# Reading the 256 activation columns of the feature-major products in turn from two halves

## The chip, the cores and the metric

The kernel runs on one core of a Trainium2 chip, in one launch. The metric is device time in microseconds, from single executions; a profile of one further execution shows which instruction ran when on each engine.

## The reference

One decoder layer on 256 tokens of width 2048, in float32:

```python
h = rms_norm(x, mix_pre_norm)
proj = h @ w_in                      # 2048 x 10536: RWKV-7, mLSTM and gate columns
merged = sigmoid(g_a) * (ha @ w_branch_a) + sigmoid(g_b) * (hb @ w_branch_b)
x = x + rms_norm(merged @ w_out, mix_post_norm)
x = x + rms_norm(cross_attention(rms_norm(x), rms_norm(mem), wq, wkv, wo), xattn_post_norm)
u = rms_norm(x) @ w_up               # 2048 x 16384, then a causal convolution over 3 tokens
x = x + rms_norm((gelu(gate) * up) @ w_down, ffn_post_norm)   # 8192 x 2048
```

Between `proj` and `merged` stand two recurrent mixers (an mLSTM and RWKV-7) of width 1024 each. Nearly all arithmetic is in the products with the weight matrices.

## The kernel before, in words

**Every large product is taken as three.** A float32 factor is split into a high part (rounded to the type fp32r) and a low part (the rest): x = xh + xl, w = wh + wl. The product is wh·xh + wh·xl + wl·xh. Activations are split once, by `split` and `split_gain` (lines 241 to 247: ScalarE makes the high part, VectorE the low one). Weights arrive by DMA on SyncE's queue in chunks of 128 partitions x 1024 columns, 512 KB each, into three buffers `raw`; `Feed.hi` makes `wh` on ScalarE (line 410) and `Feed.lo` makes `wl` on VectorE (line 432), each into one of four buffers.

**Two kinds of block.** In an "fm" (feature-major) block a 128x128 tile of weights is the stationary operand and the activations of all 256 tokens, 128x256, are the moving one; the result has features on partitions and tokens along the columns. Each product of 256 columns thus has a weight load of 128 columns of its own. A block has mostly 512 output columns: four tiles m, three products each, for each of 16 slices k of the input features. In a "tm" (token-major) block 128 tokens are the stationary operand and 512 weight columns the moving one (`tm_products`, line 436). The tm products read their 512 columns in turn from two halves already: `rearrange("p (a b) -> p b a", a=2)`, and the columns are paired on the host so that the result is in the natural order. The fm products read their 256 columns one after the other.

The fm blocks are: the small RWKV and gate columns (w_sm, 384 columns), r, k, v, q and the two gates (16 blocks of w_in), the two branches (8, with 8 slices k), w_mix_out (4), the keys and queries of the cross-attention (2), its output (4, with 4 slices k) and the feed-forward's first matrix (32). That is 144 + 54 x 192 + 8 x 96 + 4 x 48 = 11472 products of 256 columns. The tm blocks are mLSTM's v and o, the cross-attention's v and the feed-forward's second matrix.

**Where a weight chunk lies.** `Feed.staged` (line 367) places an fm chunk 16 elements into its buffer. In every second chunk ahead of the feed-forward's first matrix (and in one of 16, later one of 64, in it) the last 128 of its 1024 columns are set a further 8 elements on. Such a chunk is made by two instructions on each engine (896 and 128 columns) in place of one; `Feed.parts` and `Feed.tile` deal with the two pieces. A tm chunk lies at the start of its buffer.

**The order of work.** All instructions are written out in one program order. `run` walks through the blocks, chunk by chunk; the conversion of the next three chunks and the DMAs of the next six are issued ahead of a chunk's products. The results of a block are taken out of PSUM by generators (`r_evac`, `gate_evac`, `fu_evac` and so on), of which `Spread.half` runs a step between the slices of later blocks, by a budget of time for VectorE and ScalarE. The row scaling of the norm, `st0.rb` and its like (one number for each token, the same on all partitions), is multiplied in there, by a VectorE instruction that reads PSUM. An exception is the queries of mLSTM and the second half of `q_evac`, where 128^-0.5 goes in with it (`scalar_tensor_tensor`).

`keep_warm` issues products of a column of ones with itself; `Stat.row` and `Stat.column` are small products for the norms.

Of the kernel before, what the change touches and what calls it, by code (L numbers as in the profile page):

```python
# [10 lines left out]
F32R = mybir.dt.float32r  # L11
# [4 lines left out]
P = 128  # L16
# [136 lines left out]
def _layer(ctx, tc, nc, d, dbg):  # L153
# [194 lines left out]
    class Feed:  # L348
        def __init__(self):
            self.src = [s for b in blocks for s in b["srcs"]]  # L350
            self.kind = [b["kind"] for b in blocks for s in b["srcs"]]
            self.raw, self.st, self.nd, self.ns, self.nl = {}, {}, 0, 0, 0

            self.sm = wsm
# [31 lines left out]
        @staticmethod  # L386
        def parts(w, *others):

            if not isinstance(w, tuple):
                return [(w,) + others]  # L390
            n = w[0].shape[1]
            f = [o if isinstance(o, tuple) else o.rearrange("p k c -> p (k c)") for o in others]
            return [(w[0],) + tuple(o[0] if isinstance(o, tuple) else o[:, 0:n] for o in f),
                    (w[1],) + tuple(o[1] if isinstance(o, tuple) else o[:, n:] for o in f)]

        @staticmethod
        def tile(w, kj, nm, m):

            if not isinstance(w, tuple):
                return w[:, kj, m * P:(m + 1) * P]  # L400
            n = (kj * nm + m) * P
            return w[1] if n == w[0].shape[1] else w[0][:, n:n + P]

        def hi(self, upto):
            while self.ns <= min(upto, len(self.src) - 1):
                self.dma(self.ns)
                r = self.raw[self.ns]
                wh = self.staged("wh", r, self.ns)
                for h, v in self.parts(wh, r):
                    nc.scalar.copy(h, v)  # L410
                self.st[self.ns] = [wh, None]
                self.ns += 1

        def first(self):

            r, wh, wl = self.raw.pop(0), self.staged("wh", self.src[0], 1), self.staged("wl", self.src[0], 1)
            nc.vector.tensor_copy(wh[:, 0], r[:, 0])
            for kj in range(2):
                x_split(0, kj)
                if kj:  # L420
                    nc.scalar.copy(wh[:, 1], r[:, 1])  # L421
                nc.vector.tensor_sub(wl[:, kj], r[:, kj], wh[:, kj])
            self.st[0] = [wh, wl]
            self.ns = self.nl = 1

        def lo(self, upto):
            self.hi(upto)
            while self.nl <= min(upto, len(self.src) - 1):
                r = self.raw.pop(self.nl)
                wl = self.staged("wl", r, self.nl)  # L430
                for l, v, h in self.parts(wl, r, self.st[self.nl][0]):
                    nc.vector.tensor_sub(l, v, h)  # L432
                self.st[self.nl][1] = wl
                self.nl += 1
# [9 lines left out]
    def run():  # L444
# [6 lines left out]
        for b in blocks:  # L451
# [14 lines left out]
            for ci, s in enumerate(b["srcs"]):  # L466
# [12 lines left out]
                for kj in range(s.shape[1]):  # L479
                    xh, xl = b["xs"](k) if kj else ahead  # L480
                    first, last = k == 0, k == nk - 1
                    if b["kind"] == "fm":
                        for m in range(nm):
                            o = banks[second * 2 + m // 2][:, m % 2]
                            a, c = feed.tile(wh, kj, nm, m), feed.tile(wl, kj, nm, m)
                            mm(o, a, xh, start=(first and m % 2 == 0), stop=False)
                            if not (b["two"] and ci == 0 and first):
                                mm(o, a, xl, start=False, stop=False)
                            mm(o, c, xh, start=False, stop=last)
                        if b["two"] and ci == 0 and first:  # L490

                            for m in range(nm):
                                mm(banks[m // 2][:, m % 2], feed.tile(wh, kj, nm, m), xl, start=False, stop=False)
# [10 lines left out]
            if nt:  # L504
# [9 lines left out]
                for g, o in enumerate(banks):  # L514
                    for si, (w, kj, xh, xl) in enumerate(steps):
# [3 lines left out]
                        for m in range(2 if b["kind"] == "fm" else 0):  # L519
                            a, c = (feed.tile(v, kj, nm, g * 2 + m) for v in w)  # L520
                            mm(o[:, m], a, xh, start=(b["bankwise"] and si == 0 and m == 0), stop=False)
                            mm(o[:, m], a, xl, start=False, stop=False)
                            mm(o[:, m], c, xh, start=False, stop=si == len(steps) - 1)
                        if si % 2:
# [62 lines left out]
    def sm_evac(ps):  # L587
# [6 lines left out]
        pr = PR()  # L594
        dve.tensor_mul(pr, ps[0], bc(st0.rb, 2))
        wa, gl = C("wa", "m0"), T2("gl")
# [4 lines left out]
        pr = PR()  # L601
        dve.tensor_mul(pr[:, 0], ps[1][:, 0], st0.rb)
        shiftmix(gl1, pr[:, 0], 26, slice(0, 32))
# [173 lines left out]
    def k_evac(hf):  # L777
        def gen(ps):
# [4 lines left out]
            for g in range(2):  # L783
                pr = PR()
                dve.tensor_mul(pr, ps[g], bc(st0.rb, 2))
                yield
# [135 lines left out]
    def v_evac(hf):  # L922
        def gen(ps):
            if hf == 0:
                M["vT"], M["vt"] = U("vT"), U("vt", [P, 2, 1024])
            for g in range(2):
                p0 = hf * 4 + g * 2
                pr = PR()
                dve.tensor_mul(pr, ps[g], bc(st0.rb, 2))
                yield  # L930
# [164 lines left out]
    def q_evac(i):  # L1095
        def gen(ps):
# [4 lines left out]
            for g in range(2):  # L1101
                o = qk[:, i * 4 + g * 2:i * 4 + g * 2 + 2]
                if i == 0:
                    dve.tensor_mul(o, ps[g], bc(st0.rb, 2))
                else:
                    dve.scalar_tensor_tensor(o, ps[g], 128 ** -0.5, bc(st0.rb, 2), op0=ALU.mult, op1=ALU.mult)
                yield
            if i == 1:
# [33 lines left out]
    def mlstm():  # L1142
# [40 lines left out]
        for k2 in range(4):  # L1183
# [5 lines left out]
            for j in range(2):  # L1189
                k = k2 * 2 + j  # L1190
                split_gain(ha[0][:, k], ha[1][:, k], q[:, j], pcol("hn", k))
            yield

    def hb_split():
# [16 lines left out]
        for p2 in range(4):  # L1211
# [17 lines left out]
            dve.tensor_mul(M["bv"][:, s2], M["bv"][:, s2], q)  # L1229
            split(hb[0][:, s2], hb[1][:, s2], M["bv"][:, s2])  # L1230
            yield


    def gate_evac(i, cb):
        def gen(ps):
            sg = [T2("sg") for _ in range(2)]
            M["sg", i, cb] = sg
            for g in range(2):
                dve.tensor_mul(sg[g], ps[g], bc(st0.rb, 2))
                act.activation(sg[g], sg[g], AF.Sigmoid)  # L1240
                yield
        return gen

    def br_evac(i, cb):
        def gen(ps):
# [5 lines left out]
            for g in range(2):  # L1251
# [4 lines left out]
                else:  # L1256
                    dve.tensor_mul(sg[g], ps[g], sg[g])
                    dve.tensor_add(sg[g], sg[g], pa)
                    split(M["mg"][0][:, s2], M["mg"][1][:, s2], sg[g])
                yield  # L1260
# [29 lines left out]
    class Residual:  # L1290
# [11 lines left out]
        def run(self):  # L1302
# [165 lines left out]
    def kx_evac(ps):  # L1468
        M["kT"] = [T2("kT") for _ in range(2)]
        for g in range(2):  # L1470
            dve.tensor_mul(M["kT"][g], ps[g], bc(stm.rb, 2))
        yield
# [65 lines left out]
    def xo():  # L1538
        M["oT"] = U("oT", [P, 2, 4, S], F32R)
        for h2 in range(2):  # L1540
            q = aux("xo", [P, 2, S])
            for j in range(2):
                h = h2 * 2 + j
                for mt in range(2):
                    mm(q[:, j], M["xv"][mt][:, h * P:(h + 1) * P], M["pT", h][:, mt], start=(mt == 0), stop=(mt == 1))
            split(M["oT"][:, 0, h2 * 2:h2 * 2 + 2], M["oT"][:, 1, h2 * 2:h2 * 2 + 2], q)
            yield
# [298 lines left out]
```

## Time and profile before

| | |
|---|---|
| median of 3 executions | 1861.94 us (1861.43 to 1862.66) |
| the profiled execution | 1859.39 us |
| its span, first to last instruction | 1857.6 us |
| TensorE, its weight loads | 1843.2 us busy (99%), 1774.6 us (96%) |
| VectorE, ScalarE, GpSimd | 1313.3 us (71%), 1034.0 us (56%), 30.6 us (2%) |
| DMA | 352.73 MB, mean 190 GB/s |

The span is the time from the first to the last instruction, and the profiled execution's own time is 1.8 us longer. Matmuls are pipelined: one is listed with 276 ns, yet the next begins some 113 ns after it. So the busy share of TensorE says only that it never stopped; what counts is the time from the start of one product to the start of the next, called the pitch below. It is got from a merged row by dividing its length by its count.

### The profile page before, as it was taken

How to read it: one execution, taken by the hardware profiler on the slowest of the kernel's cores; microseconds unless marked ns; L12 is line 12 of the kernel's file. 1: busy time of each engine (PE TensorE's matmuls, PEld its weight loads, DVE VectorE, ACT ScalarE, POOL GpSimd, SP SyncE). 2: the span in 40 equal slices, each digit the busy share in tenths (PEclk: the TensorE clock that was granted, in tenths of full speed). 3: DMA queues.
4: the chain of work that ended last, by engine and by line, in shares of the span. 5: the costliest groups of instructions: out<-in, count | busy, mean ns of one | idle time of the engine just before them, and what ended most of it. 6: DMA issues, size and time to landing. Idle time of an engine off the chain costs nothing.

```text
span 1857.6 us, 36660 instructions
## 1 busy us (share of the span) xinstructions
PE 1843.2 (99%) x15038; PEld 1774.6 (96%) x15038; DVE 1313.3 (71%) x1957; ACT 1034.0 (56%) x1619; POOL 30.6 (2%) x53
## 2 busy tenths in 40 slices
PE   9999999999999999999999999999999999999998
PEld 9999988999999999899999999999999998888887
DVE  6879985765765767768777777666677676666665
ACT  6687455554544665665555655554554455555553
POOL 0100000100100000000000000000000000000000
PEclk9999999999999999999999999999999999999999
DMA  7656555354556675545666566666666666666664
GB/s 255 195 180 182 161 186 154 111 175 148 175 181 203 222 245 174 190 143 186 200 198 195 188 193 196 200 193 195 193 194 193 193 192 207 225 204 204 204 204 159
DMA packets 97913, 352.73 MB, mean 190 GB/s; under 512 B 11057, under 2 KB 11313, under 8 KB 97361
## 3 DMA queue, kind: packets, MB, share of 16 engines
q1 hardware_dynamic: 96496, 348.07, 59.9%
q8 instruction: 117, 1.92, 0.4%
q0 software_dynamic: 384, 1.18, 0.3%
q10 hardware_dynamic: 864, 1.15, 0.2%
q14 instruction: 52, 0.42, 0.1%
HBM read 347.73 MB, written 2.10 MB: 188 GB/s over the span
## 4 chain that ended last, share of the span: by engine, by line
PE 95%; DVE 3%; issue 1%; ACT 0%; DMA 0%; POOL 0%; DVEq 0%; POOLq 0%; SPq 0%; ACTq 0%
PE fm L188 68%; PE tm L188 23%; DVE wl L432 1%; PE gram L188 0%; PE Y L188 0%; DVE ql L66 0%; PE lv L188 0%; DVE z L66 0%; PE num L188 0%; PE X L188 0%; PE zwa L188 0%; DMA wsm<-in_w_sm_dram 0%; PE U L188 0%; PE gramA L188 0%; PE xo L188 0%
## 5 line engine op out<-in xcount | busy, mean ns | idle before, releaser
L432 DVE TENSOR_TENSOR wl<-raw,wh 128x1024 fp32r<-128x1024 f32 (+2 forms) x756 | 789.1, 1058 | 416.2 <-ACT wh L410 413.5
L410 ACT CAST wh<-raw 128x1024 fp32r<-128x1024 f32 (+2 forms) x756 | 678.7, 915 | 511.6 <-PE fm L188 332.0
L188 PE MATMUL fm<-fh,wh 128*128 128x256 f32 x2048 | 565.6, 276 | 0.6 <-ACT fh L66 0.6
L188 PE MATMUL fm<-fh,wl 128*128 128x256 f32 x2048 | 565.8, 276 | 0.4 <-DVE wl L432 0.4
L188 PE MATMUL fm<-fl,wh 128*128 128x256 f32 x2048 | 564.9, 276 | 0.0
L188 PEld LDWEIGHTS fm<-fh,wl 128*128 128x128 f32 x2048 | 384.5, 188 | 1.0 <-DVE wl L432 0.6
L188 PEld LDWEIGHTS fm<-fh,wh 128*128 128x128 f32 x2048 | 384.5, 188 | 0.8 <-ACT fh L66 0.8
L188 PEld LDWEIGHTS fm<-fl,wh 128*128 128x128 f32 x2048 | 384.3, 188 | 0.0
L188 PE MATMUL tm<-wh,as 128*128 128x512 f32 x1024 | 304.6, 379 | 0.0
L188 PE MATMUL fm<-hh,wh 128*128 128x256 f32 x1072 | 301.3, 281 | 1.3 <-ACT wh L421 1.3
L188 PE MATMUL fm<-hh,wl 128*128 128x256 f32 x1072 | 297.8, 278 | 0.3 <-DVE wl L432 0.2
L188 PE MATMUL fm<-hl,wh 128*128 128x256 f32 x1072 | 297.6, 278 | 0.0
L188 PEld LDWEIGHTS tm<-wh,as 128*128 128x128 f32 x1024 | 193.5, 189 | 27.4
L188 PEld LDWEIGHTS fm<-hh,wh 128*128 128x128 f32 x1072 | 201.6, 188 | 3.4 <-ACT hh L66 1.6
L188 PEld LDWEIGHTS fm<-hh,wl 128*128 128x128 f32 x1072 | 201.6, 188 | 0.7 <-DVE wl L432 0.4
L188 PEld LDWEIGHTS fm<-hl,wh 128*128 128x128 f32 x1072 | 201.7, 188 | 0.2
L188 PE MATMUL tm<-wl,as 128*128 128x512 f32 x512 | 194.0, 379 | 0.0
L188 PEld LDWEIGHTS tm<-wl,as 128*128 128x128 f32 x512 | 96.8, 189 | 13.7
L66 ACT CAST as<-ac 128x256 fp32r<-128x256 f32 x128 | 45.5, 403 | 103.7 <-PE tm L188 103.7
L66 DVE TENSOR_TENSOR as<-ac,as 128x256 fp32r<-128x256 f32 x128 | 48.6, 422 | 52.6 <-ACT as L66 52.5
L188 PE MATMUL fm<-mgh,wh 128*128 128x256 f32 x256 | 71.0, 277 | 0.0
L188 PE MATMUL fm<-mgh,wl 128*128 128x256 f32 x256 | 70.9, 277 | 0.0
(361 smaller groups left out, 2150.2 us busy)
## 6 DMA issues: line engine op xcount, KB each, us to landing
raw<-in_w_fu_dram SPq DMA_DIRECT2D x256, 512.0 KB, 4.2
raw<-in_w_in_dram SPq DMA_DIRECT2D x160, 512.0 KB, 3.9
raw<-in_w_fd_dram SPq DMA_DIRECT2D x128, 512.0 KB, 4.1
raw<-in_w_br_dram SPq DMA_DIRECT2D x32, 512.0 KB, 4.0
raw<-in_w_mo_dram SPq DMA_DIRECT2D x32, 512.0 KB, 4.2
raw<-in_w_xk_dram SPq DMA_DIRECT2D x8, 512.0 KB, 4.3
raw<-in_w_xq_dram SPq DMA_DIRECT2D x8, 512.0 KB, 3.6
raw<-in_w_xv_dram SPq DMA_DIRECT2D x8, 512.0 KB, 3.9
```

What stands on the lines that cost most here:

```text
L66: return f(out, *a, **k)
L188: pe.matmul(out, lhsT, rhs, start=start, stop=stop, skip_group_check=True)
L410: nc.scalar.copy(h, v)
L432: nc.vector.tensor_sub(l, v, h)
```

## The change

The moving operand of the fm products is read in turn from two halves of 128 columns (`turns`): columns 0, 128, 1, 129 and so on. For the result to have its tokens in the natural order, either the activations are stored so that the even tokens lie in the first half and the odd ones in the second, or the result is put in order when it is taken out of PSUM. Where activations are made for fm products alone (the branches' inputs, the merged mixers, the residual stream's splits, the attention's output) their splits read the source with a step of two elements and write one half after the other (`xsplit`, `xsplit_gain`, `Residual.parts`). The first norm's output `hh`, `hl` and the memory's `mh`, `ml` also serve the tm products, so they stay in the natural order and the evacuations of their fm products reorder (`times`). The feed-forward's evacuation `fu_evac` is untouched, since its input comes from `Residual.parts`. In `q_evac` both halves go by `times`, and the factor 128^-0.5 moves to the later product with `pw`. Weight chunks lie at the start of their buffer, in one piece; `parts`, `tile` and the list `kind` are gone.

```diff
+    def halves(ap):
+        return ap.rearrange("p k (b a) -> p k a b" if len(ap.shape) == 3 else "p (b a) -> p a b", a=2)
+    def apart(ap):
+        return ap.rearrange("p k (a b) -> p k a b" if len(ap.shape) == 3 else "p (a b) -> p a b", a=2)
+    def turns(ap):
+        return ap.rearrange("p (a b) -> p b a", a=2)
+    def xsplit(hi, lo, src):
+        split(apart(hi), apart(lo), halves(src))
+    def xsplit_gain(hi, lo, src, g):
+        split_gain(apart(hi), apart(lo), halves(src), g)
+    def times(out, ps, row):
+        if len(ps.shape) == 3:
+            row = bc(row, ps.shape[1])
+        dve.tensor_mul(apart(out), halves(ps), apart(row))
...
-        def staged(self, name, r, i):
+        def staged(self, name, r):
+            w = wp.tile([P, 1024 + 128], F32R, tag=name, bufs=4, name=name)
             k, c = r.shape[1:]
-            up = i - len(self.src) + 384
-            o = gap = 0
-            if self.kind[i] == "fm":
-                o = 16
-                if up < 0:
-                    gap = 0 if i % 2 else 8
-                elif i % (16 if up < 80 else 64) == 0:
-                    gap = 8
-            w = wp.tile([P, 1024 + 128], F32R, tag=name, bufs=4, name=name)
-            if gap:
-                n = o + k * c - P
-                return w[:, o:n], w[:, n + gap:n + gap + P]
-            return w[:, o:o + k * c].rearrange("p (k c) -> p k c", k=k)
+            return w[:, 0:k * c].rearrange("p (k c) -> p k c", k=k)
...
-                for h, v in self.parts(wh, r):
-                    nc.scalar.copy(h, v)
+                nc.scalar.copy(wh, r)
...
-                for l, v, h in self.parts(wl, r, self.st[self.nl][0]):
-                    nc.vector.tensor_sub(l, v, h)
+                nc.vector.tensor_sub(wl, r, self.st[self.nl][0])
...
                     if b["kind"] == "fm":
+                        xh, xl = turns(xh), turns(xl)
...
-                dve.tensor_mul(pr, ps[g], bc(st0.rb, 2))
+                times(pr, ps[g], st0.rb)
...
-                    dve.tensor_mul(M["pw"][:, h], M["pw"][:, h], q)
+                    dve.scalar_tensor_tensor(M["pw"][:, h], q, 128 ** -0.5, M["pw"][:, h], op0=ALU.mult, op1=ALU.mult)
...
-                split_gain(ha[0][:, k], ha[1][:, k], q[:, j], pcol("hn", k))
+                xsplit_gain(ha[0][:, k], ha[1][:, k], q[:, j], pcol("hn", k))
...
-                    act.activation(hi[:, k], part(xr, i)[:, j], AF.Identity, scale=pcol(gname, k))
+                    act.activation(apart(hi[:, k]), halves(part(xr, i)[:, j]), AF.Identity, scale=pcol(gname, k))
...
-                    dve.scalar_tensor_tensor(lo[:, k], part(xr, i)[:, j], pcol(gname, k), hi[:, k],
+                    dve.scalar_tensor_tensor(apart(lo[:, k]), halves(part(xr, i)[:, j]), pcol(gname, k), apart(hi[:, k]),
                                              op0=ALU.mult, op1=ALU.subtract)
```

The other evacuations (`sm_evac`, `k_evac`, `v_evac`, `q_evac`, `gate_evac`, `kx_evac`) and splits (`hb_split`, `br_evac`, `xo`) change in the same way.

More of the change, by code (lines that the diff above doesn't have):

```diff
@@ L350, in __init__ @@
             self.src = [s for b in blocks for s in b["srcs"]]
-            self.kind = [b["kind"] for b in blocks for s in b["srcs"]]
             self.raw, self.st, self.nd, self.ns, self.nl = {}, {}, 0, 0, 0
@@ L365, in dma @@
                 self.nd += 1
-        def staged(self, name, r, i):
+        def staged(self, name, r):
+            w = wp.tile([P, 1024 + 128], F32R, tag=name, bufs=4, name=name)
             k, c = r.shape[1:]
-            up = i - len(self.src) + 384
-            o = gap = 0
-            if self.kind[i] == "fm":
-                o = 16
-                if up < 0:
-                    gap = 0 if i % 2 else 8
-                elif i % (16 if up < 80 else 64) == 0:
-                    gap = 8
-            w = wp.tile([P, 1024 + 128], F32R, tag=name, bufs=4, name=name)
-            if gap:
-                n = o + k * c - P
-                return w[:, o:n], w[:, n + gap:n + gap + P]
-            return w[:, o:o + k * c].rearrange("p (k c) -> p k c", k=k)
[L386 to L402, printed above, removed]
+            return w[:, 0:k * c].rearrange("p (k c) -> p k c", k=k)
         def hi(self, upto):
@@ L414, in first @@
         def first(self):
-            r, wh, wl = self.raw.pop(0), self.staged("wh", self.src[0], 1), self.staged("wl", self.src[0], 1)
+            r, wh, wl = self.raw.pop(0), self.staged("wh", self.src[0]), self.staged("wl", self.src[0])
             nc.vector.tensor_copy(wh[:, 0], r[:, 0])
@@ L482, in run @@
                     if b["kind"] == "fm":
+                        xh, xl = turns(xh), turns(xl)
                         for m in range(nm):
                             o = banks[second * 2 + m // 2][:, m % 2]
-                            a, c = feed.tile(wh, kj, nm, m), feed.tile(wl, kj, nm, m)
+                            a, c = (w[:, kj, m * P:(m + 1) * P] for w in (wh, wl))
                             mm(o, a, xh, start=(first and m % 2 == 0), stop=False)
@@ L492, in run @@
                             for m in range(nm):
-                                mm(banks[m // 2][:, m % 2], feed.tile(wh, kj, nm, m), xl, start=False, stop=False)
+                                mm(banks[m // 2][:, m % 2], wh[:, kj, m * P:(m + 1) * P], xl, start=False, stop=False)
                     else:
@@ L519, in run @@
                         for m in range(2 if b["kind"] == "fm" else 0):
[L520 to L523, printed above, removed]
+                            a, c = (v[:, kj, (g * 2 + m) * P:(g * 2 + m + 1) * P] for v in w)
+                            mm(o[:, m], a, turns(xh), start=(b["bankwise"] and si == 0 and m == 0), stop=False)
+                            mm(o[:, m], a, turns(xl), start=False, stop=False)
+                            mm(o[:, m], c, turns(xh), start=False, stop=si == len(steps) - 1)
                         if si % 2:
@@ L594, in sm_evac @@
         pr = PR()
-        dve.tensor_mul(pr, ps[0], bc(st0.rb, 2))
+        times(pr, ps[0], st0.rb)
         wa, gl = C("wa", "m0"), T2("gl")
@@ L601, in sm_evac @@
         pr = PR()
-        dve.tensor_mul(pr[:, 0], ps[1][:, 0], st0.rb)
+        times(pr[:, 0], ps[1][:, 0], st0.rb)
         shiftmix(gl1, pr[:, 0], 26, slice(0, 32))
@@ L784, in gen @@
                 pr = PR()
-                dve.tensor_mul(pr, ps[g], bc(st0.rb, 2))
+                times(pr, ps[g], st0.rb)
                 yield
@@ L928, in gen @@
                 pr = PR()
-                dve.tensor_mul(pr, ps[g], bc(st0.rb, 2))
+                times(pr, ps[g], st0.rb)
                 yield
@@ L1102, in gen @@
                 o = qk[:, i * 4 + g * 2:i * 4 + g * 2 + 2]
[L1103 to L1106, printed above, removed]
+                times(o, ps[g], st0.rb)
                 yield
@@ L1229, in hb_split @@
             dve.tensor_mul(M["bv"][:, s2], M["bv"][:, s2], q)
-            split(hb[0][:, s2], hb[1][:, s2], M["bv"][:, s2])
+            xsplit(hb[0][:, s2], hb[1][:, s2], M["bv"][:, s2])
             yield
@@ L1238, in gen @@
             for g in range(2):
-                dve.tensor_mul(sg[g], ps[g], bc(st0.rb, 2))
+                times(sg[g], ps[g], st0.rb)
                 act.activation(sg[g], sg[g], AF.Sigmoid)
@@ L1258, in gen @@
                     dve.tensor_add(sg[g], sg[g], pa)
-                    split(M["mg"][0][:, s2], M["mg"][1][:, s2], sg[g])
+                    xsplit(M["mg"][0][:, s2], M["mg"][1][:, s2], sg[g])
                 yield
@@ L1470, in kx_evac @@
         for g in range(2):
-            dve.tensor_mul(M["kT"][g], ps[g], bc(stm.rb, 2))
+            times(M["kT"][g], ps[g], stm.rb)
         yield
@@ L1545, in xo @@
                     mm(q[:, j], M["xv"][mt][:, h * P:(h + 1) * P], M["pT", h][:, mt], start=(mt == 0), stop=(mt == 1))
-            split(M["oT"][:, 0, h2 * 2:h2 * 2 + 2], M["oT"][:, 1, h2 * 2:h2 * 2 + 2], q)
+            xsplit(M["oT"][:, 0, h2 * 2:h2 * 2 + 2], M["oT"][:, 1, h2 * 2:h2 * 2 + 2], q)
             yield
```

4 lines of the change are left out of this document (2 added, 2 removed).

## The prediction

> **What bounds the kernel now.** I read the page first, then the chain of waits in order of time, then the groups by form, then short stretches of the timeline.
>
> ```profile
> PE 1843.2 (99%) x15038; PEld 1774.6 (96%) x15038; DVE 1313.3 (71%) x1957; ACT 1034.0 (56%) x1619; POOL 30.6 (2%) x53
> ...
> PEclk9999999999999999999999999999999999999999
> ...
> PE 95%; DVE 3%; issue 1%; ACT 0%; DMA 0%; POOL 0%; DVEq 0%; POOLq 0%; SPq 0%; ACTq 0%
> ```
>
> The chain that ended last is TensorE for 95%, at its full granted clock throughout. So the time is the number of products times their pitch, plus about 5% of waits. The chain, in order of time, gives the pitch by stage (start, length, what, count):
>
> ```profile
> 35.32 37.24 PE fm L188 x324
> ...
> 354.96 20.73 PE fm L188 x180
> ...
> 519.15 145.24 PE fm L188 x1272
> ...
> 818.50 44.05 PE fm L188 x384
> ...
> 896.93 620.97 PE fm L188 x5470
> 1517.90 327.65 PE tm L188 x1518
> ```
>
> The feed-forward's fm products go at 620.97/5470 = 113.5 ns. The four pieces before it sum to 247.26 us for 2160, 114.5 ns, with single pieces up to 115.2. The tm products, of twice the columns, go at 327.65/1518 = 215.8 ns, and half of that is 107.9. So 256 columns cost an fm product at least 5.6 ns more than they cost a tm product. Two things differ: an fm product has a weight load for every 256 columns, not 512, and it reads its columns in sequence, where the tm product reads in turn from two halves.
>
> The matmul's own length tells something too (mean ns of one):
>
> ```profile
> L188 PE MATMUL fm<-fh,wl 128*128 128x256 f32 x2048 | 565.8, 276 | 0.4 <-DVE wl L432 0.4
> L188 PEld LDWEIGHTS fm<-fh,wl 128*128 128x128 f32 x2048 | 384.5, 188 | 1.0 <-DVE wl L432 0.6
> ...
> L188 PE MATMUL tm<-wl,hh 128*128 128x512 f32 x128 | 48.5, 379 | 0.0
> ...
> L188 PEld LDWEIGHTS tm<-wl,hh 128*128 128x128 f32 x128 | 24.2, 189 | 3.4
> ```
>
> The load is as long beside a product that reads in turn (189) as beside one that reads in sequence (188): reading in turn does not hold up the load. And these tm rows have the operands of the fm blocks with the roles changed, hh as weights and wl moving, with wl at the start of its buffer.
>
> **Do load and moving read disturb each other?** At the tile that is set 8 elements apart (matmul starts, in a w_in block):
>
> ```profile
> 158.70 0.28 PE L188 MATMUL fm<-hh,wl 128*128 128x256 f32 x1
> 158.81 0.28 PE L188 MATMUL fm<-hh,wh 128*128 128x256 f32 x1
> 158.93 0.28 PE L188 MATMUL fm<-hl,wh 128*128 128x256 f32 x1
> 159.06 0.28 PE L188 MATMUL fm<-hh,wl 128*128 128x256 f32 x1
> 159.18 0.28 PE L188 MATMUL fm<-hh,wh 128*128 128x256 f32 x1
> 159.29 0.28 PE L188 MATMUL fm<-hl,wh 128*128 128x256 f32 x1
> ```
>
> The steps are 110, 120, 130, 120, 110 ns, and such a bump returns every 48 products, that is two chunks. Only the place of the weights changes there, so where the weights lie against the moving read sets the pitch. My reading: a sequential read goes through its 256 columns at twice the rate of a load through its 128, so the two cross while both run; read in turn, the moving operand goes through two ranges of 128 columns, at the rate of the load, and does not cross it.
>
> The Trainium skill, "TensorE: Matmul & The Clock Gate", section "Step-by-step: what each phase is for", says that the moving operand and the weight load have independent read ports and that loading takes nothing from the running matmul. By that rule nothing would be there to gain (the third case below); the bump speaks against it.
>
> **What is left when they no longer cross** is the load alone or the 256 columns alone, whichever is longer. The load alone shows where a product has one moving column; the pair, where both operands are one broadcast column:
>
> ```profile
> 319.25 0.97 PEld L188 LDWEIGHTS den<-ones,pw 128*128 128x128 f32 x8
> ...
> 816.82 1.06 PE L188 MATMUL warm<-ones 128*128 128x128 f32 x8
> ...
> 259.93 1.04 PE L981 MATMUL bkt<-con,BK 128*128 128x128 f32 x8
> ```
>
> Eight loads in 0.97 us with 0.19 for the last: 0.78/7 = 111.4 ns. The eight warm products, with some 0.27 for the last, 0.79/7 = 113 ns (rows are rounded to 10 ns, so 111 to 114). The transposes, 0.77/7 = 110 ns. I take **111.5 ns**, the load's own row, as the new pitch. The bounds are 107.9 (half a tm product, no load in the way) and 113.5 (nothing gained).
>
> **The change part by part, against the profiled execution's 1859.39 us.**
>
> Pitch. There are 144 + 54 x 192 + 8 x 96 + 4 x 48 = 11472 fm products by the blocks. Of these 5470 at 113.5 come to 111.5: 5470 x 2.02 = 11.0 us. The other 6002 at 114.5: 6002 x 2.97 = 17.8 us. Nothing lies beside them that would hide this, since they are the chain. Together -28.9 us. Products of tm blocks and of the mixers stay.
>
> Chunks in one piece.
>
> ```profile
> L432 DVE TENSOR_TENSOR wl<-raw,wh 128x1024 fp32r<-128x1024 f32 x524 | 640.3, 1223 | 341.6 <-ACT wh L410 339.6 <-PE fm L188 1.2
> ...
> L432 DVE TENSOR_TENSOR wl<-raw,wh 128x896 fp32r<-128x896 f32 x116 | 126.4, 1089 | 74.6 <-ACT wh L410 73.8
> ...
> L410 ACT CAST wh<-raw 128x128 fp32r<-128x128 f32 x116 | 34.1, 294 | 0.0
> L432 DVE TENSOR_TENSOR wl<-raw,wh 128x128 fp32r<-128x128 f32 x116 | 32.9, 284 | 0.0
> ```
>
> 116 chunks save 1089 + 284 - 1223 = 150 ns on VectorE, 17 us in all, and on ScalarE somewhat under the 294 of its second piece. This lies beside TensorE; I count it as nothing, at most 1 us where VectorE is late (below).
>
> Reordering. The changed instructions read or write with a step of 8 bytes, which no row shows. The rows bound it:
>
> ```profile
> L66 ACT COPY Lt<-L x2: 1122/1128/1134, 255.3 to 257.2; 128x512 f32<-128x512 f32 x2
> ...
> L66 ACT CAST mgh<-sg 128x512 fp32r<-128x512 f32 x8 | 5.0, 622 | 20.4 <-DVE sg L66 20.4
> ...
> L66 DVE TENSOR_TENSOR mt<-cmt,con 128x256 f32<-128x256 f32 x8 | 5.1, 631 | 0.0
> ...
> L66 DVE SCALAR_TENSOR_TENSOR ql<-xr,par,qh 128x256 fp32r<-128x256 f32 x16 | 7.1, 479 | 0.2 <-ACT qh L66 0.2
> ...
> 36.00:218.00 182.00, 182.00 (x1651) 179.44 (x1650) 156.04 (x279) 117.82 (x200) 12.76 (x21) 1.00 0.61 180
> ...
> 720.00:766.00 46.00, 45.66 (x375) 44.46 (x373) 40.94 (x67) 28.54 (x47) 0.70 (x1) 1.00 0.56 175
> ```
>
> With a step of 128 bytes a ScalarE copy of 512 takes 1128 ns against 622, and a VectorE product of 256 that reads so takes 631, 152 more than ql's 479. So each 256 elements cost between 0 and some 250 ns more. 8 bytes are nearest to the contiguous rows: I take 0. On VectorE 49 instructions of 512 change (35 `times`, 14 splits) and 41 of 256: at the dear end 49 x 0.5 + 41 x 0.25 = 35 us over the kernel, less the 17 saved. TensorE covers that wherever VectorE has room. In these windows (busy us of PE, PEld, DVE, ACT, POOL with counts) VectorE has 156 of 182 us in r, k and v. It lacks room only from 720 to 766 us: 40.9 busy of 46, and there stand 16 ql and 2 kT. Dear, these add 20 x 0.25 = 5 us, and VectorE (46) would pass TensorE (45.7, less 1): a loss of 1 to 3 us. If VectorE is late, the waiting wl holds the product queue of TensorE. `oT`'s first split runs beside the second half of its own xo products, 1.9 us of cover against 1.3 now.
>
> The factor moved in `q_evac` swaps one VectorE form for another, four times; nothing. No DMA and no wait is added; each chunk's DMAs are issued at the same place.
>
> Sum: 1859.4 - 28.9 = 1830.5 us. The median of before is 2.55 us above its profiled execution, so 1833 us against the median.
>
> **The rivals.**
>
> *The 256 columns bound, not the load.* Then the pitch is between 107.9 and 110, take 109: 5470 x 4.5 + 6002 x 5.5 = 57.6 us, 1804 us. For it: the transposes' 110. Against: their load is another row than fp32r's, and den's 111.4 is the closest to an fm load.
>
> *Nothing to gain in the steady pitch.* If 113.5 is the load of these weights itself, only the bumps go: 6002 x 0.97 = 5.8 us, 1856 us, and with dear reordering it is within the measurement. For it: warm's 113. Against: den.
>
> *Slower: the new place is a bad one.* Without the 16 elements and the steps of 8, the weights may lie so that load and moving read hinder each other all along. The products of the mixer's gate, whose operands lie elsewhere, show such a pitch:
>
> ```profile
> 502.56 0.40 PE L188 MATMUL zg<-gs,gwh 128*128 128x256 f32 x2
> ...
> 503.52 0.28 PE L188 MATMUL fm<-hh,wh 128*128 128x256 f32 x1
> ```
>
> Eight in 0.96 us, 120 ns. All fm products so: 5470 x 6.5 + 6002 x 5.5 = 68.6 us, 1931 us. It decides from a mean pitch of 114 upward. Against it stand the tm rows above, read in turn with wl at the start of its buffer, 379 and 189 ns.
>
> *Slower still: each column of the other half pays.* A matmul whose columns cost double is there:
>
> ```profile
> 321.66 1.03 PE L188 MATMUL num<-vm,pw 128*128 128x256 f32 x4
> ```
>
> With 0.38 for the last, 0.65/3 = 217 ns; for 11472 products 1.18 ms more, about 3.0 ms. The tm products jump between halves 1024 bytes apart and pay nothing at 215.8 for 512; the fm halves are 512 bytes apart, which no row shows. The Trainium skill, "SBUF — State Buffer", section "Door 1: The DMA port swizzle", says that an access that leaves its 16-byte line pays; by that rule every column would. The tm rows contradict it here.
>
> **How the numbers follow.** Forecast 1833 us: 0.53. Columns bound: 0.13. Only the bumps: 0.16. A bad place: 0.15. Doubled columns: 0.03. The first three hold 0.82, so the range goes from 1803 to 1859, which takes in dear reordering (+3 on 1856). A measurement of this kernel can tell about 0.2%, 3.7 us. Faster by more: 0.53 + 0.13 + 0.11 of the third = 0.77; the rest of it, 0.05, within; slower 0.18.
>
> **What would show it.** The feed-forward's row of the chain: 5470 products in 610 us if right, 621 if nothing is gained, 656 if the place is bad. Matmuls of fm listed with fewer than 276 ns, and no bumps. The wl group has one form, 640 of 1024 columns near 1223 ns. Rows of `sg`, `pr` and `ql` near 684, 683 and 479 ns say that reordering is free. The stretch around 720 to 766 us would show VectorE on the chain if not. I am wrong if the pitch stays while loads become shorter, or if the load's row grows above 192.

## The result and the profile after

| | before | after |
|---|---|---|
| median (4 executions each) | 1862.0 us | 1838.92 us (1838.59 to 1839.28) |
| ratio | | 0.9876, 95% interval 0.9859 to 0.9893 |
| profiled execution, its span | 1859.39, 1857.6 us | 1839.28, 1837.5 us |

The change saves 1.2%, some 23 us; the two profiled executions are 20.1 us apart, and the accounts below go by these.

First the page of the kernel after: busy time by engine, and the chain that ended last.

```profile
PE 1821.2 (99%) x15038; PEld 1752.7 (95%) x15038; DVE 1305.5 (71%) x1838; ACT 1025.9 (56%) x1500; POOL 30.6 (2%) x53
...
PE 95%; DVE 2%; issue 1%; ACT 1%; DMA 0%; POOL 0%; DVEq 0%; POOLq 0%; SPq 0%; ACTq 0%
```

The same number of matmuls, nearly the same shares: over the whole span nothing else became the bound. The chain in order of time has nearly the same pieces as before:

```profile
34.91 36.18 PE fm L188 x324
...
349.38 20.30 PE fm L188 x180
...
510.12 142.05 PE fm L188 x1272
...
808.71 43.35 PE fm L188 x384
...
892.03 605.72 PE fm L188 x5422
1497.75 327.65 PE tm L188 x1518
```

The fm products go at 605.72/5422 = 111.7 ns in the feed-forward, from 113.5. At 36.18/324 = 111.7 ns and 142.05/1272 = 111.7 ns the early blocks, from 114.9 and 114.2, now have the same pitch: there are no bumps left. The piece of 384 has 112.9, with breaks in it. The one of 180 has 112.8 by length and count, but its products start 111 or 112 ns apart all through; its length takes in the end of the last one. The tm piece is the same to 0.01 us.

The groups by form that answer to those of before (busy us, mean ns of one):

```profile
L422 DVE TENSOR_TENSOR wl<-raw,wh 128x1024 fp32r<-128x1024 f32 x640 | 780.8, 1223 | 405.8 <-ACT wh L401 399.3
...
L188 PE MATMUL fm<-fh,wl 128*128 128x256 f32 x2048 | 563.5, 275 | 0.8 <-DVE wl L422 0.8
...
L188 PEld LDWEIGHTS fm<-fh,wl 128*128 128x128 f32 x2048 | 393.3, 192 | 1.4 <-DVE wl L422 1.4
...
L66 DVE TENSOR_TENSOR sg<-fm,st_b 128x512 f32<-128x512 f32 x16 | 10.9, 684 | 0.1
L66 DVE TENSOR_TENSOR pr<-fm,st_b 128x512 f32<-128x512 f32 x13 | 8.9, 683 | 0.0
L66 ACT ACTIVATE qh<-xr,par 128x256 fp32r<-128x256 f32 x16 | 8.8, 593 | 10.7 <-DVE xr L66 10.7
L66 DVE SCALAR_TENSOR_TENSOR ql<-xr,par,qh 128x256 fp32r<-128x256 f32 x16 | 7.4, 499 | 0.3 <-ACT qh L66 0.3
L66 ACT CAST mgh<-sg 128x512 fp32r<-128x512 f32 x8 | 6.3, 792 | 21.2 <-DVE sg L66 21.2
```

Three readings. The load is listed with 192 ns in place of 188, which is also the length of most loads of `den` before; this alone does not say that the load is the bound now, as the run in sequence below shows. The evacuations that reorder what they read from PSUM (`sg`, `pr`) cost the same as before: their two lines stand in the view of before with the same figures. The splits that reorder from SBUF are dearer on ScalarE (`mgh` 792 against 622) and hardly on VectorE (`ql` 499 against 479).

### The profile page after: what moved, and what is told of

Read it like the earlier page. It is cut to its first block, busy times and chain, and to the rows that moved or that the text cites. A ratio compares the mean times of both kernels' runs of the same rounds, so it can differ in the third digit from the quotient of the medians.

```text
span 1837.5 us, 36430 instructions
## 1 busy us (share of the span) xinstructions
PE 1821.2 (99%) x15038; PEld 1752.7 (95%) x15038; DVE 1305.5 (71%) x1838; ACT 1025.9 (56%) x1500; POOL 30.6 (2%) x53
## 4 chain that ended last, share of the span: by engine, by line
PE 95%; DVE 2%; issue 1%; ACT 1%; DMA 0%; POOL 0%; DVEq 0%; POOLq 0%; SPq 0%; ACTq 0%
PE fm L188 67%; PE tm L188 23%; DVE wl L422 1%; PE gram L188 0%; PE Y L188 0%; DVE ql L66 0%; PE lv L188 0%; PE num L188 0%; ACT wh L401 0%; PE X L188 0%; PE zwa L188 0%; DMA wsm<-in_w_sm_dram 0%; PE U L188 0%; PE gramA L188 0%; DMA raw<-in_w_xv_dram 0%
## 5 line engine op out<-in xcount | busy, mean ns | idle before, releaser
L422 DVE TENSOR_TENSOR wl<-raw,wh 128x1024 fp32r<-128x1024 f32 x640 | 780.8, 1223 | 405.8 <-ACT wh L401 399.3
L401 ACT CAST wh<-raw 128x1024 fp32r<-128x1024 f32 x640 | 667.1, 1045 | 502.2 <-PE fm L188 281.7
L188 PEld LDWEIGHTS fm<-fh,wl 128*128 128x128 f32 x2048 | 393.3, 192 | 1.4 <-DVE wl L422 1.4
L188 PEld LDWEIGHTS fm<-fh,wh 128*128 128x128 f32 x2048 | 393.4, 192 | 0.1
L188 PEld LDWEIGHTS fm<-fl,wh 128*128 128x128 f32 x2048 | 393.0, 192 | 0.0
L188 PEld LDWEIGHTS fm<-hh,wh 128*128 128x128 f32 x1072 | 206.5, 193 | 3.3 <-ACT hh L66 1.5
L188 PEld LDWEIGHTS fm<-hh,wl 128*128 128x128 f32 x1072 | 206.6, 193 | 0.2 <-DVE wl L413 0.2
L188 PEld LDWEIGHTS fm<-hl,wh 128*128 128x128 f32 x1072 | 206.5, 193 | 0.1
```

The costliest lines, as they stand in the source:

```text
L188: pe.matmul(out, lhsT, rhs, start=start, stop=stop, skip_group_check=True)
L401: nc.scalar.copy(wh, r)
L422: nc.vector.tensor_sub(wl, r, self.st[self.nl][0])
```

## The experiments

The theory: the sequential moving read and the weight load hinder each other by an amount that depends on where the weights lie; in turn from two halves they do not, and then the load alone sets the pitch. Rivals: the gain comes from the chunks' new place or from their being in one piece; the 256 columns, not the load, set the new pitch. All of these run on the changed kernel with the edit shown. Except for two, each time is that of a single execution; the kernel before, executed beside them, has medians from 1859.5 to 1861.5 us.

### In sequence at the new place

```diff
-        return ap.rearrange("p (a b) -> p b a", a=2)
+        return ap.rearrange("p (a b) -> p b a", a=1)
```

(and the same in `halves` and `apart`)

> The changed kernel, but the fm products read their 256 columns in sequence again (one part in place of two halves; splits and evacuations in natural order); chunks stay in one piece at the start of their buffer. If reading in turn is what helps, the fm pitch goes back to 113.4 ns at least, and, without the 16 elements and the steps of 8, perhaps to the 117 to 123 ns of the bumps: 1860 us or more, up to 1930. If the chunks' place or their being in one piece is what helps, the pitch stays near 111.7 ns: 1839 us.

Measured: 1926.98 us, 88 us above the changed kernel and 66 above the kernel before. The feed-forward's piece of the chain:

```profile
898.62 686.87 PE fm L188 x5724
```

and two groups by form:

```profile
L188 PE MATMUL fm<-fh,wl 128*128 128x256 f32 x2048 | 579.4, 283 | 0.0
...
L188 PEld LDWEIGHTS fm<-fh,wl 128*128 128x128 f32 x2048 | 393.3, 192 | 0.0
```

686.87/5724 = 120.0 ns, and each matmul is listed 7 ns longer than before. So the new place is a bad one for a sequential read, and the whole gain is the reading in turn. The load is listed with 192 ns here too, though loads follow each other 120.0 ns apart: its length does not tell what bounds. The 16 elements and the steps of 8 of the kernel before did something: without them its fm products would go much as in this run.

### In turn at the old place

The class `Feed` and the calls of `tile` are those of before; the rest is the changed kernel.

> The changed kernel with the old place of the chunks (16 elements in, last tile 8 further on in every second chunk of the early blocks, made in two pieces). If reading in turn makes the place irrelevant, the fm pitch is 111.7 ns with no bumps: 1839 us, or 1 to 2 us more where VectorE is late. If the place matters still, bumps of 117 to 123 ns come back every 48 products: 1845 us or more.

Measured: 1838.72 us, the same as the changed kernel. The feed-forward's piece:

```profile
891.50 605.72 PE fm L188 x5422
```

605.72 us for 5422, to the digit that of the changed kernel, and over all stages the products go at 111 or 112 ns with no bump. So with the halves in turn it makes no difference at which of the two places the weights lie. And making 116 chunks in two pieces costs nothing on the chain. (On VectorE it is 17 us by the listed lengths, but the busy time of its `wl` group is only 7.4 us longer, 788.2 against 780.8 us.)

### In sequence, 16 elements in

```diff
-            return w[:, 0:k * c].rearrange("p (k c) -> p k c", k=k)
+            return w[:, 16:16 + k * c].rearrange("p (k c) -> p k c", k=k)
```

(on top of the run in sequence)

> As the run in sequence, but the fm chunks (and here the tm chunks too) lie 16 elements into their buffer, with no last tile set apart. If the 16 elements are what kept the sequential read at 113.4 ns before, the undisturbed feed-forward shows 113.4 ns again where the run at the start of the buffer shows more. If not, both show the same pitch.

Measured: 1884.73 us. The feed-forward's piece of the chain:

```profile
898.45 644.78 PE fm L188 x5470
```

117.9 ns in the feed-forward: better than at the start of the buffer (120.0) and worse than before (113.5). So the 16 elements are a part of it, and the last tile set 8 elements apart the larger one. In the trace of this run some stretches stay at 113 and others at 118 ns, as this piece of earlier blocks (113.4 ns) beside the one above:

```profile
520.80 111.45 PE fm L188 x983
```

It happens within one block too: in the feed-forward the products start 113 ns apart until a wait at 904 us, and 118 ns apart from there to the end. So this read has two steady states, and there nothing brings it back to the better one. I had read the bumps of before as a cost of the step of 8. By the starts in the trace of before they also put the pitch back: after the one at 129 us it stays at 118 ns, and the next, at 135.6 us, puts it back to 113.

### Short products, short loads

```diff
-                                mm(o, a, xl, start=False, stop=False)
+                                mm(o[:, 0:P], a, xl[:, 0:64], start=False, stop=False)
```

> The changed kernel, where the product wh times xl takes only 128 of its 256 columns (the low part of half the tokens' activations is left out; the blocks that are done bank by bank keep theirs). One third of the fm products then streams half as long. If the weight load sets the pitch of 111.7 ns, nothing changes: 111.7 ns for all three products, 1839 us. If the 256 columns set it, the short ones fall towards 56 ns: some 3700 products x 50 ns, 180 us less.

Measured: 1838.47 us, no difference. The groups by form:

```profile
L188 PE MATMUL fm<-fh,wl 128*128 128x256 f32 x2048 | 671.7, 328 | 0.9 <-DVE wl L422 0.8
L188 PE MATMUL fm<-fl,wh 128*128 128x128 f32 x2044 | 453.8, 222 | 0.0
...
L188 PEld LDWEIGHTS fm<-fl,wh 128*128 128x128 f32 x2048 | 393.0, 192 | 0.0
```

and the feed-forward's piece of the chain:

```profile
891.22 605.72 PE fm L188 x5422
```

One third of the products stream half as long, and 5422 of them still take 605.72 us: what the short product leaves free, the next one takes longer (328 ns in place of 275). So the 256 columns do not set the pitch.

```diff
-                                mm(o, a, xl, start=False, stop=False)
+                                mm(o[0:64], a[:, 0:64], xl, start=False, stop=False)
```

> The changed kernel, where the product wh times xl loads only 64 of its 128 weight columns (the low part's product is left out for half the features; the blocks that are done bank by bank keep theirs). If the load sets the pitch, the step that waits for the short load falls from 111.7 ns to what 256 columns take alone, 108 to 110 ns, one third of the products: 3700 x 2 to 4 ns, 7 to 14 us less. If the columns set it already, nothing changes: 1839 us.

Measured: 1829.89 us, 9.0 us less. The short load's group by form:

```profile
L188 PEld LDWEIGHTS fm<-fl,wh 128*64 128x64 f32 x2044 | 282.1, 138 | 0.0
```

and the feed-forward's piece of the chain:

```profile
887.20 601.20 PE fm L188 x5422
```

601.20/5422 = 110.9 ns on average. With two steps at 111.7 the third, the one that waits for the short load, is at 109.2; the starts in the trace agree, with two steps of three at 111 or 112 ns and one at 109 or 110. So the load sets the pitch and the 256 columns would allow 109.2: 2.5 ns per product are left, for whoever finds a way to load less often. I did not find one.

### Why two halves?

My theory had a mechanism: two halves make the moving read go through its places at the load's rate, so that they never cross. Four kernels test it.

```diff
-        return ap.rearrange("p (a b) -> p b a", a=2)
+        return ap.rearrange("p (a b) -> p b a", a=4)
```

(and in `halves` and `apart`)

> Four quarters in turn in place of two halves (columns 0, 64, 128, 192, 1, 65 and so on), splits with a step of four. If what matters is only that load and moving read do not run at different rates through the same places, two halves are special: with quarters the moving read goes at half the load's rate, they cross again, and the pitch is above 111.7 ns, 113 or more. If it matters only that neighbouring columns come from different places, quarters do as well: 111.7 ns in the feed-forward, with ScalarE's and VectorE's splits of step 16 bytes dearer than those of step 8 (qh 593 ns, ql 499 ns).

Measured: 2153.63 us. The feed-forward's piece of the chain:

```profile
1026.04 786.10 PE fm L188 x5724
```

and the group of one form:

```profile
L188 PE MATMUL fm<-fh,wl 128*128 128x256 f32 x2048 | 618.4, 302 | 0.0
```

786.10/5724 = 137.3 ns in the feed-forward, far above the sequential read, and 143.3 in the early blocks (185.76 us for 1296). In turn is not good as such.

```diff
-        return ap.rearrange("p (a b) -> p b a", a=2)
+        return ap.rearrange("p (h a b) -> p h b a", h=2, a=2)
```

(here and in the next two with a=1 in `halves` and `apart`, so without any reordering)

> The changed kernel with another order of reading: first columns 0 to 127 in turn from their halves of 64 (0, 64, 1, 65 and so on), then columns 128 to 255 the same way. Activations are stored and results taken out in the natural order, so the tokens of every fm result stand in another order than the reference's; the work is the same. Two places at a time, 256 bytes apart, each gone through at the load's rate; the quarters had four places, 256 bytes apart, each at half that rate. If two places at the load's rate are what counts, the pitch is 111.7 ns. If 256 bytes apart is what made the quarters dear, it is 130 ns or more. If the jump in the middle meets the load, something between, 113 to 125 ns.

Measured: 1836.46 us; its feed-forward piece is again 605.72 us for 5422, 111.7 ns. So places 256 bytes apart, the quarters' distance, are not what made them dear.

```diff
-        return ap.rearrange("p (a b) -> p b a", a=2)
+        return ap[:, 0:P].unsqueeze(2).broadcast_to((P, P, 2))
```

> No reordering, and the fm products read the first 128 columns in sequence, each twice in a row (0, 0, 1, 1 and so on); the other half of the tokens is left out and the first half stands twice. One place only, gone through at the load's rate. If the rate is what counts, one place does as well as two: 111.7 ns, 1836 to 1839 us. If it is that neighbouring columns come from different places, the pitch is that of the sequential read at this place, 120 ns: 1925 us.

Measured: 1840.64 us, 111.7 ns. One place at the load's rate does as well as two: that neighbouring columns come from different places is not the point.

```diff
-        return ap.rearrange("p (a b) -> p b a", a=2)
+        return ap.rearrange("p (a b) -> p b a", a=2)[:, 0:64].unsqueeze(2).broadcast_to((P, 64, 2, 2))
```

> No reordering, and the fm products read two places in turn, each column pair twice (0, 128, 0, 128, 1, 129 and so on up to 63 and 191); half of the tokens is left out and the others stand twice. Two places, each gone through at half the load's rate, as the quarters' four were. If the rate is what made the quarters dear, the pitch is above 111.7 ns here too, 115 to 143. If it is the number of places, 111.7 ns.

Measured: 1836.68 us, 111.7 ns. Here the equal rate falls: two places at half the load's rate are just as good. What the six orders show together is a pattern without its cause:

| order of reading | places | rate of each against the load | pitch in the feed-forward |
|---|---|---|---|
| in sequence | 1 | twice | 113.4 to 120.0 ns, by the weights' place |
| each column twice | 1 | same | 111.7 |
| halves; two by 64 | 2 | same | 111.7 |
| two, each pair twice | 2 | half | 111.7 |
| quarters | 4 | half | 137.3 |

In these six, an order is free when it goes through no place faster than the load goes through its own, and through one or two places at a time. Why four are dear, and what the sequential read meets, was not settled; three places, or quarters at another place of the weights, were not tried. The two orders that repeat columns also read half as many different ones, which may help them.

### Where the rest of the forecast went

The forecast was 8.8 us too good against the profiled execution. Put side by side, the same pieces of both chains show two stretches where the gain disappears. Up to the piece of 1272 products the kernel after is 519.15 - 510.12 = 9.03 us ahead. The next piece starts at 667.80 before and at 658.06 after, 9.74 ahead: 1272 products, each 2.5 ns faster, are 3.2 us, and 0.7 came through. This is the first stretch. The second begins there: the piece of 384 starts at 818.50 before and at 808.71 after, 9.79 ahead, so of 983 products' gain 0.05 us came through. The chain of that second stretch has, beside products, conversions of weights and a wait for a chunk of the cross-attention's v, before (3.55 us) and after (4.25):

```profile
759.86 3.55 DMA raw<-in_w_xv_dram
```

```profile
749.13 4.25 DMA raw<-in_w_xv_dram
```

No run changed that stretch alone, so its cause is open. The first one was looked into. The chain of the kernel after in it (start, length, engine and tile):

```profile
652.17 0.85 DVE wl L422
...
654.71 2.35 DVE wl L422 x2
...
658.06 9.49 PE fm L188 x84
```

ScalarE's wait just ahead of this (in the brackets at the end),

```profile
651.10 1.05 ACT L401 CAST wh<-raw 128x1024 fp32r<-128x1024 f32 x1 [3.75 <-DMA raw<-in_w_mo_dram]
```

and the kernel's stretches of 5 us (length, then busy us with counts of PE, PEld, DVE, ACT and POOL, the granted clock, the DMA share and GB/s):

```profile
645.00:650.00 5.00, 5.00 (x48) 5.00 (x47) 3.75 (x5) 2.35 (x5) 0.00 (x0) 1.00 1.00 384
650.00:655.00 5.00, 4.19 (x35) 3.81 (x34) 2.83 (x5) 3.90 (x6) 0.00 (x0) 1.00 0.53 203
655.00:660.00 5.00, 3.72 (x33) 3.53 (x32) 3.69 (x5) 1.69 (x3) 0.41 (x1) 1.00 0.73 238
```

TensorE waits for `wl`, VectorE for `wh`, and ScalarE had stood 3.75 us before it for its chunk of weights (2.91 us in the kernel before), while the DMA engines were full at 384 GB/s. Here `load_x` fetches the residual stream again, 2 MB ahead of the weight chunks, with the memory tokens just before. Before, the DMA engines were full as well, a little later, and TensorE, slower, did not run out meanwhile; it lost some three products' time just behind (43 from 665 to 670 us, where 46 is usual; the same view of the kernel before):

```profile
650.00:655.00 5.00, 5.00 (x46) 5.00 (x46) 2.92 (x5) 5.00 (x11) 0.00 (x0) 1.00 1.01 385
655.00:660.00 5.00, 5.00 (x47) 5.00 (x46) 4.14 (x7) 2.89 (x6) 0.00 (x0) 1.00 1.00 368
...
665.00:670.00 5.00, 4.93 (x43) 4.73 (x42) 3.43 (x6) 2.21 (x5) 0.71 (x1) 1.00 0.78 233
```

My reading: the transfers of this stretch take their time whatever TensorE does, and a faster TensorE waits for them. Two ways out were tried.

```diff
-            sp.dma_start(M["xr"][i], d["x"][:, i * 8:i * 8 + 8])
+            act.dma_start(M["xr"][i], d["x"][:, i * 8:i * 8 + 8])
```

> The changed kernel, where the residual stream's 2 MB are loaded again (load_x, beside w_mix_out) through ScalarE's DMA queue in place of SyncE's, where they stand ahead of the weight chunks. If the 4 to 5 us that the stretch from 510 to 710 us lost against the forecast are the wait of ScalarE for a weight chunk behind that load (3.75 us), the wait shrinks and the kernel takes 1835 to 1838 us. If the sixteen DMA engines are what is short there, the chunk comes as late as before: 1839 us.

Measured over 4 executions: 1839.23 us (1839.11 to 1840.0), ratio to before 0.9884 (0.987 to 0.990): nothing. Through another queue the transfers were no sooner done: the piece of 84 products starts at 658.64 us, after 658.06 in the changed kernel. The chain of this run has a chunk of w_mix_out on it for 10.2 us:

```profile
638.87 10.20 DMA raw<-in_w_mo_dram
```

and in the 5 us at whose end it lands the DMA engines are nearly full (0.92, 373 GB/s):

```profile
645.00:650.00 5.00, 4.92 (x45) 4.73 (x43) 0.89 (x1) 0.85 (x1) 0.00 (x0) 1.00 0.92 373
```

```diff
-        for i in range(2):
-            sp.dma_start(M["xr"][i], d["x"][:, i * 8:i * 8 + 8])
+
+    def x_again(b):
+        def pre(ci, feed):
+            i = (b - 1) * 8 + ci
+            sp.dma_start(M["xr"][i // 8][:, i % 8:i % 8 + 1], d["x"][:, i:i + 1])
+        return pre
...
-              before=load_x if b == 1 else None)
+              before=load_x if b == 1 else None, pre=x_again(b) if b in (1, 2) else None)
```

> The changed kernel, where the residual stream's 2 MB are loaded again in 16 pieces of 128 KB, one with each chunk of w_mix_out's second and third block, in place of two of 1 MB at the start of the second. The DMA engines were full (share 1.00, 384 GB/s) from 645 to 650 us, and ScalarE waited 3.75 us for a weight chunk. If that is where the forecast's last part went, the wait goes and the kernel takes 1834 to 1836 us. If VectorE's own work is what is late there, 1838 to 1839 us.

Measured over 4 executions: 1835.84 us (1835.38 to 1837.52), ratio to before 0.9865 (0.9848 to 0.9881), some 3 us below the changed kernel. Its stretches of 5 us:

```profile
645.00:650.00 5.00, 5.00 (x48) 5.00 (x47) 5.00 (x8) 4.61 (x9) 0.00 (x0) 1.00 0.70 222
650.00:655.00 5.00, 5.00 (x48) 5.00 (x46) 3.65 (x5) 2.83 (x3) 0.00 (x0) 1.00 0.92 310
655.00:660.00 5.00, 5.00 (x46) 5.00 (x46) 3.12 (x4) 3.04 (x5) 0.72 (x1) 1.00 0.90 285
```

TensorE no longer stops there. This is the fastest of the kernels that do the whole work; the intervals of its ratio and of the changed kernel's overlap, and what sets them apart is that 4 of 4 executions are below all 4 of the other.

### Without any reordering

`halves` and `apart` with a=1, `turns` with a=2.

> The changed kernel without any reordering: halves in turn as in the changed kernel, but activations stored and results taken out in the natural order, so the tokens of every fm result stand in another order than the reference's; the work is the same. Pitch 111.7 ns. If the dearer splits (qh 593 against 503 ns, mgh 792 against 622, ql 499 against 479) cost nothing on the chain, the time is 1838 to 1839 us; if the stretch from 710 to 760 us pays for them, 1836 to 1837 us.

Measured: 1836.51 us, 2.4 us below the changed kernel. It is a single execution, but two of the runs above that do not reorder either have 1836.46 and 1836.68 us; the third, each column twice, has 1840.64, and its first long piece starts 2.4 us late (37.35 us against 34.91). So reordering seems to cost some 2 us on the chain. They arise in the first stretch, not in the one from 710 to 760 us that I named: at the start of the long piece near 510 us this run is 0.14 us ahead (509.98 against 510.12), and by the next piece of 360 products it is 2.29 ahead of the changed kernel:

```profile
665.70 40.20 PE fm L188 x360
```

```profile
667.99 40.20 PE fm L188 x360
```

So this gain and that of the reload in pieces come from the same place; whether they add up was not tried.

## Why the prediction was right, step by step

**The pitch of 111.5 ns: right.** Measured 111.7. It was taken from the load's row where nothing else bounds, and the two runs with short products and short loads show that this was the right row: the load sets the pitch, the columns alone would give 109.2. The rival of 109 ns was thus the next bound, not this one.

**The reason for it: not borne out.** The prediction's reading was that halves go through their columns at the load's rate and so never cross it. Two places at half that rate are as good (111.7 ns), and four, at the same half rate, are not (137.3). That the hindrance would go was forecast rightly, and the tm rows were evidence for it; the reason I gave was not the right one, and the right one is open.

**The bad place: right as a mechanism, not for this kernel.** The price of 120 ns and 1931 us is what the sequential read costs at the new place (120.0 ns, 1927 us). The tm rows, which spoke against it for a read in turn, were the right evidence. The Trainium skill's statement that the load takes nothing from the running matmul ("TensorE: Matmul & The Clock Gate", "Step-by-step: what each phase is for") does not fit these sequential reads: 113.5, 117.9 and 120.0 ns go with three places of the weights.

**The doubled columns: not so.** The Trainium skill's rule that leaving a 16-byte line costs ("SBUF — State Buffer", "Door 1: The DMA port swizzle") would make halves pay at every column; they pay nothing that the pitch of 111.7 ns shows. Quarters, which leave it too, pay at 137.3, far from the 217 of that rival.

**The sum: mis-sized.** Forecast 28.9 us, measured 20.1 (by the medians 1833 and 1838.92 us). The feed-forward's term was 11.0; its 5470 products went from 620.97 us to 611.65 (886.10 to 1497.75), 9.3. The pitch was 0.2 ns higher, 1 us, and the 113.5 had some waits in it, which stayed. The term of the other 6002 products was 17.8, and 20.1 - 9.3 = 10.8 came. By stages, with the fm products counted in the traces:

| stage, by its end before | products | forecast at 2.97 ns each | came |
|---|---|---|---|
| to 519.15 us | 3050 | 9.1 us | 9.0 us |
| to 667.80 us, the first stretch | 1295 | 3.8 | 0.7 |
| to 818.50 us, the second stretch | 983 | 2.9 | 0.05 |
| to 896.93 us | 674 | 2.0 | 1.0 |

So up to 519 us the term was right. The step that failed behind it is the sentence that nothing lies beside the products that would hide the gain, since they are the chain: from there to the feed-forward transfers and conversions of weights lie beside them, and of some 8.8 us 1.8 came. In the first stretch the DMA engines took some 3 us back, as the reload in pieces shows; I looked for VectorE to be late, not for a stretch in which transfers alone set the time. What took the gain in the other two was not tested.

**The chunks in one piece at nothing: right** (1838.92 us, and 1838.72 with two pieces). The 17 us that I gave VectorE for it are 8.3 in busy time (the `wl` group, 789.1 to 780.8 us). **Reordering at nothing: nearly.** PSUM reads cost nothing (683 and 684 ns); the SBUF splits got dearer, mostly on ScalarE, and the whole cost some 2 us. I had given 1 to 3 as the dear end, but for another stretch (720 to 766 us) and for VectorE, so that the numbers meet is luck.

**A sign that was badly chosen.** I wrote that a load's row above 192 would prove me wrong. It rose to 192, and in some groups to 193, while the forecast pitch came; and the sequential read at 120.0 ns has 192 too. The row does not tell the cases apart.

## What to carry to other kernels

Where each matmul has a weight load of its own, find the pitch of the load alone (products of one column show it) and compare: what lies above it is hindrance or columns, and which of the two it is shows in how the pitch moves with the weights' place. Reading the moving operand in turn from two halves took the hindrance away at both places tried, so that no offsets had to be found; four parts were far worse, so try before going further. And when the bound gets faster, look for the stretches where transfers or other engines lie beside it: there the gain can vanish, and here spreading one large load over the chunks beside it gave back 3 us.

## What the runs showed of the hardware that I had not expected

A VectorE product that reads PSUM with a step of 8 bytes is as fast as without (683 and 684 ns for 512). A ScalarE cast that reads SBUF with that step is not: 792 against 622 ns for 512. Reading in turn from four parts in place of two raised the pitch from 111.7 to 137.3 ns. And a sequential read can stay in one of two steady pitches, 113 and 118 ns, within one block and with the weights at one place.
